# A one-layer decoder trunk: gates and branch projections with the tokens stationary, and squares and sums issued later

## The chip, the cores and the metric

One Trainium2 chip, one NeuronCore of it. The metric is the device time of one execution in microseconds, median of three runs. Inputs and outputs are float32.

## The reference, cut to what matters

One layer, 256 tokens, 2048 channels (`D_MODEL`), FFN width 5632. The mixer has two branches: A is gated linear attention over chunks, B a gated causal convolution with LayerNorm. Both are projected to 2048 channels, weighted by sigmoid gates computed from the input, added and projected once more.

```python
branch_a = (o * jax.nn.silu(r)) @ w_o_gla
...
u = jax.nn.silu(_layernorm(u, conv_norm_g, conv_norm_b))
branch_b = u @ w_pw2 + b_pw2
g_a, g_b = jnp.split(gates, 2, axis=-1)
merged = jax.nn.sigmoid(g_a) * branch_a + jax.nn.sigmoid(g_b) * branch_b
return merged @ w_out
...
h = h + _mixer(_rmsnorm(h, norm_mix[l]), ...)
h = h + (jax.nn.silu(y @ w_gate) * (y @ w_up)) @ w_down     # y = _rmsnorm(h, norm_ffn[l])
return _rmsnorm(h, norm_final)
```

## The kernel before, in words

**Split operands.** Every float32 operand of a large matmul is split into a high part (rounded to fp32r by ScalarE, line 194 or 815) and the rest (`lo`, a subtraction on VectorE, line 196 or 818); a product is hi·hi + lo·hi + hi·lo.

**Blocks of the mixer.** `run_blocks` (line 203) goes through the weight matrices in blocks of 512 output columns. A block has 16 row blocks of 128 input channels (K), loaded in 8 chunks of two. There are three forms of a product:

- Form "M" (lines 243 and 244): the weights are stationary, 128 columns at a time; the tokens stream. For each row block and each of four column groups there is one matmul of 512 columns (high and low part of the tokens, side by side) and one of 256 columns. The result has channels on partitions, and its two halves are added later (`merged_sum`, line 262: a ScalarE copy and a VectorE sum).
- Form "A" (lines 235 to 237): 128 tokens are stationary, 512 weight columns stream, three matmuls for each row block and each half of the tokens. The result has tokens on partitions. Before the change only the value projection uses it.
- Form "S" is for the narrow decay projection.

The order is: convolution values and gates (8 blocks), decay, keys, queries, values (4 blocks, form A), output gate `r` (4), gate A (4), gate B (4), branch A's projection (4, tokens `OG`, tile name `ogs`), branch B's projection (4, tokens `US`, tile `us`), output projection (4, tokens `MG`, tile `mgs`).

**What runs beside them.** Loading a chunk, and its cast and subtraction, are issued four chunks ahead (`LOOK`) by `load_next` (line 168); the weight loads go out on SP's queue. The element-wise work of attention and convolution waits in two lists, `gla_w_` and `conv_w_` (class `Work`, line 114). After each chunk `pump` (line 146) issues steps from them up to a budget. A step may have a delay in chunks, counted from the last step that its list issued (lines 126 and 127). Instructions here are not held in the written order: a scheduler places them by its own model of when their inputs are ready; `issue_after` only says behind which instruction a step may not come. Instructions wrapped in `kp` (`keep_in_program_order`) are held in order.

**The merge.** The gates' evacuation (`pair_evac`, line 485) applies the sigmoid; `o_evac` (line 688) multiplies branch A's projection by gate A; `pw_evac` (line 696) adds branch B's bias, multiplies by gate B, adds, and splits the merged channels (`MG`). The output projection reads row block k of `MG` in chunk k/2. `out_before` (line 708) closes the mixer's tile pools, opens the FFN's and loads the residual `XR` on SP's queue. `out_evac` (line 720) adds the residual, scales by the norm's gain, splits, and for every pair of 128-channel groups forms token sums (`token_sums`, line 769) and adds up squares (lines 738 to 743); at the end it folds them (line 747).

**The FFN.** It runs in steps of four row blocks of weights (`steps`, line 794): 88 for gate and up, 44 for down, most of them 24 matmuls of 512 columns with tokens stationary (lines 1228 to 1230); "S" steps use a seven-product scheme with more additions on VectorE. `run_ffn` (line 1185) writes the order out by hand: `vt["p"]` and `vt["d"]` model the time of TensorE and VectorE, `pump_d` (line 977) issues evacuations and preparations of later steps (a step has two halves, each with its cast and subtraction) when VectorE's modelled time is behind, and `turns` holds transposes with due times. `h2_norm` (line 1081) needs the folded squares; `h2_turn` (line 1090) transposes the residual, four 128x128 blocks at a time, through TensorE (line 1095). The down projection has two passes (`q` 0 and 1) over 1024 output columns each. At the end of a bank `dn_evac` (line 1102) adds the result to the residual (1105), squares it with a row sum on ScalarE (1108) and multiplies it by the final gain (1112).

Of the kernel before, what the change touches and what calls it, by code (L numbers as in the profile page):

```python
# [13 lines left out]
P = 128  # L14
T = 256
# [12 lines left out]
NPERS = 16  # L28
# [13 lines left out]
def trunk(ctx: ExitStack, tc, xT, par, convw, ws, wal2, nfin, out):  # L42
# [27 lines left out]
    def ptile(dt=F32, s="p"):  # L70
        return pers.tile([P, NB], dt, tag="p", name=nm(s))
# [87 lines left out]
    def add_block(width, nk, form, xs, evac, before=None, budget=BUD):  # L159
        blocks.append(dict(width=width, nk=nk, form=form, xs=xs, evac=evac,  # L160
                           before=before, budget=budget))
# [41 lines left out]
    def run_blocks():  # L203
# [11 lines left out]
        for b in blocks:  # L215
# [115 lines left out]
    def x_scaled(k):  # L331
        def f():
            s = ptile(F32R, "xs")
# [345 lines left out]
    MG = {}  # L679
# [7 lines left out]

    def o_evac(blk):
        def f(n, a):
            i = 4 * blk + n  # L690
            t = merged_sum(a)
            g = SGA[i // 2][:, i % 2, :]
            v.tensor_tensor(g, t, g, op=ALU.mult)
        return f

    def pw_evac(blk):
        def f(n, a):
            i = 4 * blk + n
            t = merged_sum(a, pcol(P_PB, i))
            u = ttile("mg")  # L700
            v.tensor_tensor(u, t, SGB[i // 2][:, i % 2, :], op=ALU.mult)
            w = ttile("mg2")
            v.tensor_tensor(w, u, SGA[i // 2][:, i % 2, :], op=ALU.add)
            MG[i] = ptile(F32R, "mgs")
            split(MG[i], w)
        return f

    def out_before(blk):
        def f():
            if blk == 0:  # L710
                mx.close()
                es = ctx.enter_context
                ffn["f"] = es(tc.tile_pool(name="fpool", bufs=NF, reuse_waits="tile"))
                ffn["x"] = es(tc.tile_pool(name="xpool", bufs=NX, reuse_waits="tile"))
            for i in range(2 * blk, 2 * blk + 2):
                XR[i] = atile([P, 2, T], s="xr")
                nc.sync.dma_start(XR[i], xT[:, 2 * i:2 * i + 2, :])
        return f

    def out_evac(blk):  # L720
        def f(n, a):
# [14 lines left out]
            if i % 2 == 1:  # L736
                token_sums(i // 2, YP.pop(i // 2))
                q = atile([P, 2, T], s="hq")
                sc.activation(q, H2[i // 2], AF.Square)
                if i > 1:  # L740
                    o = atile([P, 2, T], s="hss")
                    v.tensor_tensor(o, sums["h"], q, op=ALU.add)
                    q = o
                sums["h"] = q
# [24 lines left out]
    def token_sums(p, y):  # L769
        kinds = {k for w, _, q, k in gu if q == p}  # L770
        parts = []
        if "S" in kinds:
            f = atile([P, 4, P], s="sf")
            v.tensor_tensor(f[:, 0], y[:, 0, H1], y[:, 1, H1], op=ALU.subtract)
            v.tensor_tensor(f[:, 1], f[:, 0], y[:, 0, H0], op=ALU.subtract)
            v.tensor_tensor(f[:, 2], y[:, 0, H0], y[:, 0, H1], op=ALU.subtract)
            v.tensor_tensor(f[:, 3], y[:, 1, H0], f[:, 1], op=ALU.add)
            SY[p] = [atile([P, 4, P], F32R, "sy") for _ in range(2)]
            parts.append((f, *SY[p]))
        if "P" in kinds:  # L780
            f = atile([P, 2, P], s="df")
            v.tensor_tensor(f, y[:, :, H0], y[:, :, H1], op=ALU.subtract)
            DY[p] = atile([P, 2, 2, P], F32R, "dy")
            parts.append((f, DY[p][:, 0], DY[p][:, 1]))
        for f, hi, lo in parts:
            sc.copy(hi, f)
            v.tensor_tensor(lo, f, hi.bitcast(F32), op=ALU.subtract)
# [186 lines left out]
    evac = deque()  # L974
    turns = deque()
# [76 lines left out]
    def back(blk, n, x):  # L1052
# [9 lines left out]
        def cut(m):  # L1062
            hi, lo = HSV[blk, n] = ptile(F32R, "hsh"), ptile(F32R, "hsl")
# [26 lines left out]
    def h2_turn(th, nb):  # L1090
        def f():
# [4 lines left out]
            HTK[th, nb] = ptile(s="htk")  # L1096
# [5 lines left out]
    def dn_evac(q):  # L1102
        def add(t, nb, a, p0=0, p1=NB, c=None):
            h = HTK[t, nb]
            kp(v.tensor_tensor(h[:, p0:p1], a[:, p0:p1], h[:, p0:p1], op=ALU.add))
            sq = atile([P, NB], s="dq")
# [64 lines left out]
        def done_bank(b, a):  # L1171
# [8 lines left out]
            else:  # L1180
                later(0.7, lambda: add(t, nb, a))
                later(0.7, lambda: scaled(t, nb))
        return done_bank

    def run_ffn():
# [8 lines left out]
        while i < len(steps):  # L1194
# [89 lines left out]
    for blk in range(4):  # L1284
        add_block(NB, KT, "M", lambda: MG, out_evac(blk), before=out_before(blk))
# [62 lines left out]
```

## Time and profile before

| | |
|---|---|
| runs shown (3) | 1658.71, 1660.85, 1661.5 us; median 1660.85 |
| profiled execution | 1658.77 us, of it the span 1657.1 us |
| mean granted TensorE clock | 0.995 |
| TensorE / VectorE / ScalarE busy | 1640.4 / 1396.8 / 931.3 us |
| instructions | 22482 |
| DMA | 340.5 MB, mean 206 GB/s |

Times in the rows below are microseconds from the start of the span. A timeline row reads: start, duration, engine and line, operation, output<-inputs, size, count, and in brackets the engine's idle time before it with what ended it. Matmuls are pipelined, and their recorded durations overlap: the rate is read from starts. [...]

### The profile page before, as it was taken

How to read it: one execution, taken by the hardware profiler on the slowest of the kernel's cores; microseconds unless marked ns; L12 is line 12 of the kernel's file. 1: busy time of each engine (PE TensorE's matmuls, PEld its weight loads, DVE VectorE, ACT ScalarE, POOL GpSimd, SP SyncE). 2: the span in 40 equal slices, each digit the busy share in tenths (PEclk: the TensorE clock that was granted, in tenths of full speed). 3: DMA queues.
4: the chain of work that ended last, by engine and by line, in shares of the span. 5: the costliest groups of instructions: out<-in, count | busy, mean ns of one | idle time of the engine just before them, and what ended most of it. 6: DMA issues, size and time to landing. Idle time of an engine off the chain costs nothing.

```text
span 1657.1 us, 22482 instructions
## 1 busy us (share of the span) xinstructions
PE 1640.4 (99%) x8397; PEld 1394.6 (84%) x8397; DVE 1396.8 (84%) x2104; ACT 931.3 (56%) x1276; POOL 23.9 (1%) x46
## 2 busy tenths in 40 slices
PE   9999999999999999999999999999999999999997
PEld 8888888888888888888888888888888888887886
DVE  7998999888888889887668868888888888888776
ACT  6654444666666654475555555555555555544554
POOL 0000000000000000000000000000000000000000
PEclk9999999999999999999999999999999999999999
DMA  8555555554444545445556546666666767884963
GB/s 296 196 203 179 197 184 178 199 182 172 175 174 167 178 170 186 178 178 204 190 204 213 172 168 222 227 219 218 224 229 228 229 228 237 280 315 162 316 227 115
DMA packets 78365, 340.54 MB, mean 206 GB/s; under 512 B 8976, under 2 KB 10256, under 8 KB 58160
## 3 DMA queue, kind: packets, MB, share of 16 engines
q1 hardware_dynamic: 75232, 329.61, 57.1%
q0 software_dynamic: 2880, 9.44, 1.6%
q8 instruction: 65, 1.06, 0.3%
q14 instruction: 44, 0.36, 0.1%
q10 hardware_dynamic: 144, 0.07, 0.0%
HBM read 327.54 MB, written 11.53 MB: 205 GB/s over the span
## 4 chain that ended last, share of the span: by engine, by line
PE 94%; DVE 3%; DMA 1%; ACT 1%; issue 1%; ACTq 0%; SPq 0%; DVEq 0%
PE acc L243 32%; PE acc L244 16%; PE m L1229 13%; PE m L1230 13%; PE m L1228 13%; PE acc L235 2%; PE acc L236 2%; PE acc L237 2%; DVE lo L818 1%; DMA raw<-in_weights_dram 1%; PE m L1059 1%; PE m L596 0%; ACT hi L815 0%; PE m L511 0%; DMA pr<-in_par_dram 0%
## 5 line engine op out<-in xcount | busy, mean ns | idle before, releaser
L194 ACT CAST hi<-raw 128x1024 fp32r<-128x1024 f32 (+1 forms) x326 | 339.0, 1041 | 340.1 <-PE acc L243 280.1
L196 DVE TENSOR_TENSOR lo<-raw,hi 128x1024 fp32r<-128x1024 f32 (+1 forms) x326 | 393.4, 1208 | 110.2 <-ACT hi L194 107.9
L243 PE MATMUL acc<-xs,hi 128*128 128x512 f32 x1280 | 452.4, 398 | 0.0
L818 DVE TENSOR_TENSOR lo<-raw,hi 128x1024 fp32r<-128x1024 f32 x264 | 317.6, 1220 | 88.2 <-ACT hi L815 87.5
L244 PE MATMUL acc<-xs,lo 128*128 128x256 f32 x1280 | 359.0, 280 | 0.0
L815 ACT CAST hi<-raw 128x1024 fp32r<-128x1024 f32 x264 | 270.5, 1050 | 149.5 <-PE m L1230 72.4
L243 PEld LDWEIGHTS acc<-xs,hi 128*128 128x128 f32 x1280 | 240.3, 188 | 57.8 <-ACT hi L194 0.3
L244 PEld LDWEIGHTS acc<-xs,lo 128*128 128x128 f32 x1280 | 241.8, 189 | 0.1
L393 DVE SCALAR_TENSOR_TENSOR yc<-u,cw,yc 128x255 f32<-128x255 f32 (+14 forms) x480 | 199.5, 463 | 0.1
L1228 PE MATMUL m<-hi,y2s 128*128 128x512 f32 x404 | 159.4, 395 | 0.9 <-ACT hi L815 0.9
L1229 PE MATMUL m<-lo,y2s 128*128 128x512 f32 x404 | 157.8, 391 | 1.0 <-DVE lo L818 1.0
L1230 PE MATMUL m<-hi,y2s 128*128 128x512 f32 x404 | 157.9, 391 | 0.0
L243 PE MATMUL acc<-xu,hi 128*128 128x512 f32 x256 | 90.9, 398 | 1.1 <-DVE xu L107 1.1
L1229 PEld LDWEIGHTS m<-lo,y2s 128*128 128x128 f32 x404 | 76.2, 189 | 16.6 <-DVE lo L818 1.3
L1228 PEld LDWEIGHTS m<-hi,y2s 128*128 128x128 f32 x404 | 76.2, 188 | 16.5 <-ACT hi L815 1.3
L243 PE MATMUL acc<-ogs,hi 128*128 128x512 f32 x256 | 89.9, 395 | 0.0
L1230 PEld LDWEIGHTS m<-hi,y2s 128*128 128x128 f32 x404 | 76.1, 188 | 16.0
L243 PE MATMUL acc<-us,hi 128*128 128x512 f32 x256 | 88.8, 391 | 0.0
L243 PE MATMUL acc<-mgs,hi 128*128 128x512 f32 x256 | 88.8, 391 | 0.0
L1228 PE MATMUL m<-hi,hr 128*128 128x512 f32 x216 | 85.3, 395 | 2.6 <-ACT hi L815 2.6
L1229 PE MATMUL m<-lo,hr 128*128 128x512 f32 x216 | 85.5, 396 | 1.3 <-DVE lo L818 1.3
L1230 PE MATMUL m<-hi,hr 128*128 128x512 f32 x216 | 85.0, 394 | 0.0
(256 smaller groups left out, 2791.6 us busy)
## 6 DMA issues: line engine op xcount, KB each, us to landing
raw<-in_weights_dram SPq DMA_DIRECT2D x157, 1024.0 KB, 4.8
raw<-in_weights_dram SPq DMA_DIRECT2D x268, 512.0 KB, 4.9
hr<-hsd SPq DMA_DIRECT2D x56, 256.0 KB, 6.7
hsd<-hsh POOLq DMA_DIRECT2D x18, 256.0 KB, 2.7
hsd<-hsl POOLq DMA_DIRECT2D x18, 256.0 KB, 3.0
raw<-in_weights_dram SPq DMA_DIRECT2D x8, 256.0 KB, 4.7
xr<-in_xT_dram SPq DMA_DIRECT2D x8, 256.0 KB, 5.4
out_dram<-fin SPq DMA_DIRECT2D x8, 256.0 KB, 3.2
```

What stands on the lines that cost most here:

```text
L194: order["a"] = sc.copy(fl(hi), r).ins
L196: order["v"] = v.tensor_tensor(fl(lo), r, fl(hi).bitcast(F32), op=ALU.subtract).ins
L235: pe.matmul(a, lhsT=xh, rhs=hi[:, kk, :], start=st, stop=False)
L236: pe.matmul(a, lhsT=xh, rhs=lo[:, kk, :], start=False, stop=False)
L243: pe.matmul(a, lhsT=wh, rhs=x, start=st, stop=False)
L244: last = pe.matmul(a[:, T:2 * T], lhsT=wl, rhs=xh, start=False, stop=en)
L393: v.scalar_tensor_tensor(y[:, d:T], in0=u_tile(i)[:, 0:T - d], scalar=cw[:, i, CW - 1 - d:CW - d], in1=y[:, d:T], op0=ALU.mult, op1=ALU.add)
L815: kp(sc.copy(dst, src))
L818: kp(v.tensor_tensor(dst, src, hi.bitcast(F32), op=ALU.subtract))
L1228: kp(pe.matmul(a, lhsT=xh, rhs=wh, start=st, stop=False))
L1229: kp(pe.matmul(a, lhsT=xh, rhs=wl, start=False, stop=False))
L1230: kp(pe.matmul(a, lhsT=xl, rhs=wh, start=False, stop=en))
```

## The change

The eight gate blocks and the eight blocks of the two branch projections go from form M to form A. The gates' sigmoid reads the accumulator directly, 512 wide; the two branches are merged with tokens on partitions. Branch B's bias, now needed along the free axis, is rearranged once by a GpSimd transfer into a DRAM row (`brow`) and broadcast to all partitions, 512 values per block. The merged result is transposed back by TensorE, four 128x128 blocks into one PSUM bank, copied by ScalarE and split by VectorE (`turn_merged`). `out_before` of the first output block is called ahead of the last two chunks instead of at the block's start. In the FFN's start the last pair's squares, the fold and the last two pairs' token sums go into a list `slow` with due times on TensorE's modelled time; in the first pass of the down projection the square and the final scaling go there too. Tiles of the long-lived pool are made twice as large and half as many.

```diff
-NPERS = 16
+NPERS = 8
...
     def ptile(dt=F32, s="p"):
-        return pers.tile([P, NB], dt, tag="p", name=nm(s))
+        return pers.tile([P, 2, NB], dt, tag="p", name=nm(s))
...
             for c in range(nch):
+                if c == nch - 2 and b["late"]:
+                    b["late"]()
...
-    MG = {}
+    class Merged(dict):
+        def __missing__(self, k):
+            gla_w_.drain(("mg", k // 4))
+            return self[k]
+    MG = Merged()
+    BP = {}
+    brow = dpool.tile([16, P], F32, tag="brow", name="brow")
+    with nc.allow_non_contiguous_dma(reason="2048 values once"):
+        nc.gpsimd.dma_start(brow, par[:, P_PB:P_PB + 16].rearrange("p i -> i p"))
+
+    def sg_evac(store):
+        def mk(blk):
+            def f(n, a):
+                store[n, blk] = atile([P, NB], s="sg")
+                sc.activation(store[n, blk], a, AF.Sigmoid)
+            return f
+        return mk
+
     def o_evac(blk):
         def f(n, a):
-            i = 4 * blk + n
-            t = merged_sum(a)
-            g = SGA[i // 2][:, i % 2, :]
-            v.tensor_tensor(g, t, g, op=ALU.mult)
+            g = SGA[n, blk]
+            v.tensor_tensor(g, a, g, op=ALU.mult)
+        return f
+
+    def pw_before(blk):
+        def f():
+            if blk == 0:
+                conv_w_.drain("conv")
+            BP[blk] = atile([P, NB], s="bp")
+            nc.sync.dma_start(BP[blk], brow[4 * blk:4 * blk + 4, :].rearrange("a b -> (a b)").partition_broadcast(P))
         return f
 
     def pw_evac(blk):
         def f(n, a):
-            i = 4 * blk + n
-            t = merged_sum(a, pcol(P_PB, i))
-            u = ttile("mg")
-            v.tensor_tensor(u, t, SGB[i // 2][:, i % 2, :], op=ALU.mult)
-            w = ttile("mg2")
-            v.tensor_tensor(w, u, SGA[i // 2][:, i % 2, :], op=ALU.add)
-            MG[i] = ptile(F32R, "mgs")
-            split(MG[i], w)
+            u = SGB[n, blk]
+            t = atile([P, NB], s="mg")
+            v.tensor_tensor(t, a, BP[blk], op=ALU.add)
+            v.tensor_tensor(u, t, u, op=ALU.mult)
+            v.tensor_tensor(u, u, SGA[n, blk], op=ALU.add)
+            if n == 1:
+                for z in range(2):
+                    turn_merged(blk, z)
+                gla_w_.mark(("mg", blk))
         return f
 
+    def turn_merged(blk, z):
+        st = {}
+
+        def t():
+            m = st["m"] = misc()
+            for j in range(2):
+                for n in range(2):
+                    pe.transpose(m[:, (2 * j + n) * P:(2 * j + n + 1) * P],
+                                 SGB[n, blk][:, (2 * z + j) * P:(2 * z + j + 1) * P], ident)
+
+        def cut():
+            mg = ptile(F32R, "mgs")
+            m = st["m"].rearrange("p (k t) -> p k t", k=2)
+            sc.copy(mg[:, :, 0:T], m)
+            v.tensor_tensor(mg[:, :, T:2 * T], m, mg[:, :, 0:T].bitcast(F32), op=ALU.subtract)
+            for j in range(2):
+                MG[4 * blk + 2 * z + j] = mg[:, j]
+        gla_w_.add(0.0, t, 1 if z else 3)
+        gla_w_.add(0.7, cut, 1)
+
     def out_before(blk):
         def f():
             if blk == 0:
+                gla_w_.drain(("mg", 3))
                 mx.close()
...
             if i % 2 == 1:
-                token_sums(i // 2, YP.pop(i // 2))
-                q = atile([P, 2, T], s="hq")
-                sc.activation(q, H2[i // 2], AF.Square)
...
-            if i == 15:
-                fo = ttile("hf")
-                v.tensor_tensor(fo, sums["h"][:, 0, :], sums["h"][:, 1, :], op=ALU.add)
-                sums["f"] = fo
+                def square():
+                    q = atile([P, 2, T], s="hq")
+                    kp(sc.activation(q, H2[i // 2], AF.Square))
...
+                def fold():
+                    sums["f"] = ttile("hf")
+                    kp(v.tensor_tensor(sums["f"], sums["h"][:, 0, :], sums["h"][:, 1, :], op=ALU.add))
+                if i < 13:
+                    token_sums(i // 2, YP.pop(i // 2))
+                if i < 15:
+                    square()
+                else:
+                    slow.extend([(1.0, square), (1.5, fold)] + [
+                        (5.0 + 3.0 * z, lambda p=p: token_sums(p, YP.pop(p))) for z, p in enumerate((6, 7))])
...
         def add(t, nb, a, p0=0, p1=NB, c=None):
             h = HTK[t, nb]
             kp(v.tensor_tensor(h[:, p0:p1], a[:, p0:p1], h[:, p0:p1], op=ALU.add))
+            if q:
+                square(t, nb, p0, p1, c)
+            else:
+                slow.append((vt["p"] + 12.0 + 6.0 * len(slow), lambda: (square(t, nb), scaled(t, nb))))
...
                 later(0.7, lambda: add(t, nb, a))
-                later(0.7, lambda: scaled(t, nb))
+                if q:
+                    later(0.7, lambda: scaled(t, nb))
...
             for z in range(len(groups[0])):
...
+                if slow and slow[0][0] <= vt["p"]:
+                    slow.popleft()[1]()
+                    vt["d"] += 0.7
...
-    ga = pair_evac(SGA, AF.Sigmoid, "sga")
+    ga, gb = sg_evac(SGA), sg_evac(SGB)
     for blk in range(4):
-        add_block(NB, KT, "M", xx, ga(blk), before=layernorm if blk == 0 else None)
-    gb = pair_evac(SGB, AF.Sigmoid, "sgb")
+        add_block(NB, KT, "A", xx, ga(blk), before=layernorm if blk == 0 else None)
     for blk in range(4):
-        add_block(NB, KT, "M", xx, gb(blk))
+        add_block(NB, KT, "A", xx, gb(blk))
     for blk in range(4):
-        add_block(NB, KT, "M", lambda: OG, o_evac(blk),
+        add_block(NB, KT, "A", lambda: OG, o_evac(blk),
...
     for blk in range(4):
-        add_block(NB, KT, "M", lambda: US, pw_evac(blk),
-                  before=(lambda: conv_w_.drain("conv")) if blk == 0 else None)
+        add_block(NB, KT, "A", lambda: US, pw_evac(blk), before=pw_before(blk))
     for blk in range(4):
-        add_block(NB, KT, "M", lambda: MG, out_evac(blk), before=out_before(blk))
+        add_block(NB, KT, "M", lambda: MG, out_evac(blk), **{"before" if blk else "late": out_before(blk)})
```

In the token sums (`token_sums`) the instructions are now wrapped in `kp`.

## Rows read from the trace of the kernel before

**Rows 1.** The page: busy time, share and instructions by engine; the chain by engine.

```profile
PE 1640.4 (99%) x8397; PEld 1394.6 (84%) x8397; DVE 1396.8 (84%) x2104; ACT 931.3 (56%) x1276; POOL 23.9 (1%) x46
...
PE 94%; DVE 3%; DMA 1%; ACT 1%; issue 1%; ACTq 0%; SPq 0%; DVEq 0%
```

**Rows 2.** Timeline of TensorE in a gate stage, form M, three pairs apart.

```profile
599.63 0.40 PE L243 MATMUL acc<-xs,hi 128*128 128x512 f32 x1
...
600.69 0.40 PE L243 MATMUL acc<-xs,hi 128*128 128x512 f32 x1
```

**Rows 3.** Timeline of TensorE: first matmul of branch A's, branch B's and the output projection.

```profile
663.59 0.40 PE L243 MATMUL acc<-ogs,hi 128*128 128x512 f32 x1
...
753.85 0.39 PE L243 MATMUL acc<-us,hi 128*128 128x512 f32 x1
...
842.60 0.39 PE L243 MATMUL acc<-mgs,hi 128*128 128x512 f32 x1
```

**Rows 4.** Timeline of TensorE in the value projection, form A, six matmuls apart.

```profile
299.68 0.39 PE L236 MATMUL acc<-lo,xs 128*128 128x512 f32 x1
...
301.04 0.39 PE L236 MATMUL acc<-lo,xs 128*128 128x512 f32 x1
```

**Rows 5.** Timeline of VectorE and TensorE where the mixer hands over to the FFN.

```profile
940.04 0.28 DVE L776 TENSOR_TENSOR sf<-yp 128x128 f32<-128x128 f32 x1
940.25 0.28 DVE L775 TENSOR_TENSOR sf<-sf,yp 128x128 f32<-128x128 f32 x1
...
941.81 0.69 DVE L787 TENSOR_TENSOR sy<-sf,sy 128x512 fp32r<-128x512 f32 x1 [0.74 <-ACT sy L786]
...
942.04 0.39 PE L1230 MATMUL m<-hi,dy 128*128 128x512 f32 x1
...
943.29 0.49 PE L1228 MATMUL m<-hi,y2s 128*128 128x512 f32 x1 [0.87 <-ACT hi L815]
...
943.48 1.22 DVE L818 TENSOR_TENSOR lo<-raw,hi 128x1024 fp32r<-128x1024 f32 x1
...
944.75 0.50 PE L1229 MATMUL m<-lo,y2s 128*128 128x512 f32 x1 [0.96 <-DVE lo L818]
```

**Rows 6.** Timeline of TensorE around four transposes; their group by line (busy, mean ns).

```profile
949.20 0.39 PE L1230 MATMUL m<-hi,y2s 128*128 128x512 f32 x1
949.43 0.60 PE L1095 MATMUL m<-ident,h 128*128 128x128 f32 x4
...
950.10 0.40 PE L1229 MATMUL m<-lo,y2s 128*128 128x512 f32 x1
...
L1095 PE MATMUL m<-ident,h 128*128 128x128 f32 x32 | 4.8, 272 | 0.0
```

**Rows 7.** Windows: length, busy PE, PEld, DVE, ACT, POOL; granted clock, DMA share, GB/s.

```profile
945.00:949.00 4.00, 4.00 (x14) 3.29 (x14) 4.00 (x4) 3.58 (x5) 0.00 (x0) 0.57 0.47 163
```

**Rows 8.** Timeline of TensorE and ScalarE between the down projection's two passes.

```profile
1525.97 0.39 PE L1230 MATMUL m<-hi,hr 128*128 128x512 f32 x1
...
1527.20 0.63 ACT L1108 ACTIVATE dq<-htk 128x512 f32<-128x512 f32 x1 [1.36 <-DVE htk L1105]
...
1527.83 1.98 ACT L815 CAST hi<-raw 128x1024 fp32r<-128x1024 f32 x2
...
1528.91 0.64 PE L1228 MATMUL m<-hi,hr 128*128 128x512 f32 x1 [2.56 <-ACT hi L815]
...
1530.17 0.80 PE L1229 MATMUL m<-lo,hr 128*128 128x512 f32 x1 [0.62 <-DVE lo L818]
```

**Rows 9.** Windows at the same place, columns as in rows 7.

```profile
1526.00:1530.00 4.00, 1.00 (x3) 0.19 (x1) 2.97 (x4) 2.60 (x4) 0.00 (x0) 0.89 0.02 7
1530.00:1536.00 6.00, 5.83 (x14) 4.57 (x15) 4.97 (x7) 3.55 (x5) 0.00 (x0) 0.51 0.58 186
```

**Rows 10.** First 25 us: the chain (start, duration); a DMA queue's packets, MB, share.

```profile
10.74 6.29 DMA raw<-in_weights_dram
...
q10 hardware_dynamic: 144, 0.07, 0.9%
```

More of the change, by code (lines that the diff above doesn't have):

```diff
@@ L70, in ptile, with phalf @@
     def ptile(dt=F32, s="p"):
-        return pers.tile([P, NB], dt, tag="p", name=nm(s))
+        return pers.tile([P, 2, NB], dt, tag="p", name=nm(s))
+    pair_of = {}
+    def phalf(i, dt=F32, s="p"):
+        if i % 2 == 0:
+            pair_of[s] = ptile(dt, s)
+        return pair_of[s][:, i % 2]
     def misc(shape=(P, 512)):
@@ L157, in trunk, with add_block @@
     blocks = []
-    def add_block(width, nk, form, xs, evac, before=None, budget=BUD):
+    def add_block(width, nk, form, xs, evac, before=None, budget=BUD, late=None):
         blocks.append(dict(width=width, nk=nk, form=form, xs=xs, evac=evac,
-                           before=before, budget=budget))
+                           before=before, budget=budget, late=late))
     loads = []
@@ L332, in f @@
         def f():
-            s = ptile(F32R, "xs")
+            s = phalf(k, F32R, "xs")
             t = ttile("xn")
@@ L736, in f @@
             if i % 2 == 1:
-                token_sums(i // 2, YP.pop(i // 2))
-                q = atile([P, 2, T], s="hq")
-                sc.activation(q, H2[i // 2], AF.Square)
[L740 to L744, printed above, removed]
-            if i == 15:
-                fo = ttile("hf")
-                v.tensor_tensor(fo, sums["h"][:, 0, :], sums["h"][:, 1, :], op=ALU.add)
-                sums["f"] = fo
+                def square():
+                    q = atile([P, 2, T], s="hq")
+                    kp(sc.activation(q, H2[i // 2], AF.Square))
+                    if i > 1:
+                        o = atile([P, 2, T], s="hss")
+                        kp(v.tensor_tensor(o, sums["h"], q, op=ALU.add))
+                        q = o
+                    sums["h"] = q
+                def fold():
[8 more added lines that the diff above has]
+                        (5.0 + 3.0 * z, lambda p=p: token_sums(p, YP.pop(p))) for z, p in enumerate((6, 7))])
         return f
@@ L773, in token_sums @@
             f = atile([P, 4, P], s="sf")
[L774 to L777, printed above, removed]
+            kp(v.tensor_tensor(f[:, 0], y[:, 0, H1], y[:, 1, H1], op=ALU.subtract))
+            kp(v.tensor_tensor(f[:, 1], f[:, 0], y[:, 0, H0], op=ALU.subtract))
+            kp(v.tensor_tensor(f[:, 2], y[:, 0, H0], y[:, 0, H1], op=ALU.subtract))
+            kp(v.tensor_tensor(f[:, 3], y[:, 1, H0], f[:, 1], op=ALU.add))
             SY[p] = [atile([P, 4, P], F32R, "sy") for _ in range(2)]
@@ L781, in token_sums @@
             f = atile([P, 2, P], s="df")
-            v.tensor_tensor(f, y[:, :, H0], y[:, :, H1], op=ALU.subtract)
+            kp(v.tensor_tensor(f, y[:, :, H0], y[:, :, H1], op=ALU.subtract))
             DY[p] = atile([P, 2, 2, P], F32R, "dy")
@@ L785, in token_sums @@
         for f, hi, lo in parts:
-            sc.copy(hi, f)
-            v.tensor_tensor(lo, f, hi.bitcast(F32), op=ALU.subtract)
+            kp(sc.copy(hi, f))
+            kp(v.tensor_tensor(lo, f, hi.bitcast(F32), op=ALU.subtract))
     gu = [("gu", b, p, "S" if p in SEVEN[b] else "P") for b in range(11) for p in range(8)]
@@ L974, in trunk @@
     evac = deque()
+    slow = deque()
     turns = deque()
@@ L1062, in cut @@
         def cut(m):
-            hi, lo = HSV[blk, n] = ptile(F32R, "hsh"), ptile(F32R, "hsl")
+            hs = ptile(F32R, "hs")
+            hi, lo = HSV[blk, n] = hs[:, 0], hs[:, 1]
             cast(hi, m)
@@ L1095, in f @@
                 kp(pe.transpose(m[:, q * P:(q + 1) * P], H2[i // 2][:, i % 2, th * P:(th + 1) * P], ident))
-            HTK[th, nb] = ptile(s="htk")
+            HTK[th, nb] = phalf(nb, s="htk")
             kp(sc.copy(HTK[th, nb], m))
@@ L1105, in add, with square @@
             kp(v.tensor_tensor(h[:, p0:p1], a[:, p0:p1], h[:, p0:p1], op=ALU.add))
+            if q:
+                square(t, nb, p0, p1, c)
+            else:
+                slow.append((vt["p"] + 12.0 + 6.0 * len(slow), lambda: (square(t, nb), scaled(t, nb))))
+        def square(t, nb, p0=0, p1=NB, c=None):
+            h = HTK[t, nb]
             sq = atile([P, NB], s="dq")
```

## The prediction

> **What bounds the kernel now.** I read the page's busy shares and its chain of waits first. TensorE is busy nearly all the span and carries 94% of the chain [rows 1]: the time is TensorE's issue time plus the few places where TensorE stands still. So I priced issue rates from the timeline of TensorE (starts of successive matmuls, since the recorded durations overlap), and then looked for its idle entries.
>
> Issue rates. In the M form a pair is one 512-column and one 256-column matmul. In the two gate stages three pairs take 1.06 us, 0.353 us a pair [rows 2]. In the branch B projection 256 pairs run from 753.85 to 842.60, 0.347 a pair [rows 3]. The kernel thus issues the same pair at two speeds; the trace does not say why. The A form already exists here, in the value projection, inside the slower of those stretches: six matmuls of 512 columns from 299.68 to 301.04, 0.2267 us each [rows 4]. Per row block of weights the two forms stream the same columns (4 x 768 = 6 x 512), but M issues 8 instructions and A 6.
>
> Standstills. There are two of any size. [...] Where the first half of the down projection ends, it waits again, at 1528.91 and 1530.17 [rows 8], and from 1530 to 1536 the granted clock is 0.51, the lower level almost throughout [rows 9].
>
> **The change part by part.** The profiled execution took 1658.77 us (span 1657.1); the median of the three runs is 1660.85, 2.1 above it. I sum against the former and add 2.1.
>
> *Sixteen blocks from M to A* (two gates, two branch projections; four blocks of sixteen row blocks each). An A block is 96 x 0.2267 = 21.76 us. The eight gate blocks: 8 x 64 x 0.353 = 180.9 becomes 174.1, a gain of 6.8. Branch B: 88.75 becomes 87.05, 1.7. Branch A: 90.26 from 663.59 to 753.85 [rows 3] becomes 87.05 plus the two small LayerNorm reductions that stand in it in both kernels; I leave 1.0 for them (bounds 0 and 1.5) and take 2.2. **Sum -10.7.**
>
> *Thirty-two transposes* of 128x128 are new, eight groups of four. The FFN already has such groups: from 949.20 to 950.10, one group between two matmuls took 0.90 us where two matmul steps alone take 0.45, so 0.45 a group [rows 6]. **+3.6.** Each group brings a ScalarE copy and a VectorE subtraction 512 wide (0.69 us, as the operation at 941.81 [rows 5]), and what they replace is more: per block the M form spent four copies, four sums and, in the last projection, four 256-wide splits. They lie under TensorE: the last projection block's channels are first read in the seventh chunk of the output projection, 6 x 2.77 = 16.6 us after the block ends (88.75 us are 32 chunks). Without that cover TensorE would wait for two groups' work, some 5 us, once.
>
> By the rows a group in the stream costs 0.45 us, though each transpose's recorded duration is 272 ns [rows 6]. [...] I follow the spacing.
>
> *Where the transposes stand on TensorE.* They read what VectorE finishes only after the block's last matmul (three 512-wide operations of 0.69 us for each token half), and the code can add them right behind that matmul: the written delay of three chunks counts from the queue's last step, which is long past. I price this at 0.5 us in all, since the program's scheduler does not keep written order: VectorE ran line 776 before line 775 [rows 5]. From below it is 0; from above see the first rival.
>
> *First standstill.* TensorE lost 1.25 + 1.45 - 0.45 = 2.25 us [rows 5], and (1 - 0.57) x 4 = 1.7 at the lower clock [rows 7]. What was late was the cast at the head of the third FFN step, which stands on ScalarE behind the squares; the subtraction stands on VectorE behind the token sums, the sum of squares and its fold (941.81 to 943.48 [rows 5]). The change puts the squares, fold and both last token sums behind that step's first half. About 3 us of VectorE work leaves the chain, so the subtraction should end near 942 where it now starts at 943.48, and TensorE needs it two matmul steps after 942.04, at 942.5. Next late would be the tiny norm matmuls, which need the fold some 1.4 us after that; VectorE has it by about 943.2. **-3.9.**
>
> *Second standstill.* The cast at 1527.83 starts as the third square with its accumulator read ends (1527.20) [rows 8]: ScalarE takes them in order, and each scaling on VectorE waits for its square too. The change leaves only the four additions there; squares and scalings come one by one 12 to 30 us later. The cast then runs as soon as it has data and a buffer. No transfer is late next: DMA was idle in that gap (share 0.02 [rows 9]). Gain: from 1525.97 to 1530.17 there are 4.2 us for two steps of 0.227, so 3.75 lost, and (1 - 0.51) x 6 = 2.9 at the lower clock. **-6.6.** The moved work, four squares of 0.63 us and four scalings of 0.69, goes under later steps of 5 us each; its cover is TensorE's stream there, without it VectorE's 2.8 us would be on the path. I count it within the 0.5 above.
>
> *The bias row.* A GpSimd transfer turns 2048 values one by one at the start, where TensorE's chain hangs on weight loads (one took 6.29 us [rows 10]). The nearest row is the parameter load: 144 packets held 0.9% of sixteen engines over 25 us, 25 ns each [rows 10]. At that price 2048 pieces take 3.2 us of every engine. From below 0 (the engines have pauses), from above 3.2 if all of it delays the loads, more if a piece costs more than a row of 512 B. I take the middle, **+1.5**. The four broadcast loads and the later x loads on SP's queue have most of a block in hand: 0.
>
> *The output projection* keeps the M form, and may run at 0.347 as now or at 0.353: 0 to 1.7 us, taken as **+0.8**.
>
> Sum: -10.7 + 3.6 + 0.5 - 3.9 - 6.6 + 1.5 + 0.8 = -14.8; 1658.8 - 14.8 = 1644.0, as a median 1646.
>
> **The rivals.**
> 1. *The transposes wait at the head of TensorE's queue* (slower). If the written order holds, each branch B block ends with TensorE waiting for the second half's three operations (2.1), what is left of the first half's (0.7, since that half ends six steps of 0.227 earlier) and perhaps a weight subtraction (1.22 [rows 5]): 4.0 us, four times. The first standstill, of 2.25 us, was followed by 1.7 us lost to the clock. 4 x 5.7 = 22.8 gives 1668. It turns the sign once the wait with its clock loss exceeds 14.8 / 4 = 3.7 us a block. For: the delay that does not bind. Against: the reordering in [rows 5].
> 2. *The second standstill stays*, because VectorE is late itself: 1646 + 6.6 = 1652.6. For: it was busy 2.97 of the 4 us around it [rows 9]. Against: the first idle entry names the cast, not VectorE [rows 8], and part of that busy time is the scalings that go.
> 3. *The start is delayed* by 2048 pieces at several times 25 ns: three times that price is 9.6 us, 8 more than counted, 1654. For: the chain there is DMA [rows 10]. Against: no row shows a dear small piece.
> 4. *Transposes at their full duration*: 1646 + 5.2 = 1651. For: the 272 ns. Against: the 0.90 us in the stream. [...]
>
> **How the numbers follow.** Forecast 0.63, rival 1 0.10, rival 2 0.14, rival 3 0.08, rival 4 0.05. A measurement of this kernel can tell about 0.2%, 3.3 us. Faster by more than that is below 1657.5: the forecast, rivals 2 and 4 and nearly all of 3, 0.88. Of rival 1, where the wait may be shorter, 0.08 is slower; what is left, 0.04, is the same. Low end: bias row, projection speed and small waits at nothing, -2.8, and 1 us for the bounds in branch A, 1642. High end 1655 takes in rivals 2 to 4 and leaves out rival 1.
>
> **What would show it.** Right: starts 0.227 apart in gates and projections; four-transpose groups at 0.45 without idle before them; no idle entry above 0.5 us where the FFN begins, nor where the second half of the down projection begins; no granted clock under 0.95 at either place. Wrong: idle entries that name VectorE before transposes; the weight load at the start that lands at 17.03 [rows 10] landing later; a wait for a cast near 1515 to 1525 in place of that at 1528.

## The result, and the profile after

The changed kernel takes **1680.74 us** (median of 4 runs, 1677.8 to 1683.3) against 1660.8 us for the kernel before: a ratio of 1.0126 with the 95% interval [1.011, 1.0142]. It is 20 us slower, where 1646 us and a range up to 1655 us were forecast. Its profiled execution took 1679.42 us (span 1677.7). All differences below are against the profiled execution of before.

The page of the changed kernel, the lines that answer to [rows 1]: busy time, share and instructions by engine, then the chain by engine.

```profile
PE 1641.9 (98%) x7917; PEld 1376.0 (82%) x7917; DVE 1377.6 (82%) x2016; ACT 908.4 (54%) x1188; POOL 25.3 (2%) x47
...
PE 91%; DVE 4%; DMA 2%; issue 1%; ACT 1%; SPq 0%; ACTq 0%; DVEq 0%
```

TensorE issues 480 instructions fewer and VectorE has less to do, as the diff says, and still the span is 20.65 us longer. TensorE's share of the chain fell from 94 to 91%, so the time went into standing still. Where it did is read from the first matmul of each stage; after − before gives what a stage gained or lost. The timeline of TensorE, changed kernel (start, duration, engine and line, operation):

```profile
10.52 0.79 PE L251 MATMUL acc<-xu,hi 128*128 128x512 f32 x1 [4.77 <-DVE xu L115]
...
111.06 0.40 PE L251 MATMUL acc<-xs,hi 128*128 128x512 f32 x1
...
670.69 0.39 PE L243 MATMUL acc<-hi,ogs 128*128 128x512 f32 x1
...
758.64 0.39 PE L243 MATMUL acc<-hi,us 128*128 128x512 f32 x1
...
865.16 0.48 PE L251 MATMUL acc<-mgs,hi 128*128 128x512 f32 x1
...
957.93 0.40 PE L1307 MATMUL m<-hi,y2s 128*128 128x512 f32 x1
...
1435.03 0.39 PE L1307 MATMUL m<-hi,hs 128*128 128x512 f32 x1
```

The third block of the first stage, which begins here at 111.06 us, began in the kernel before at:

```profile
98.20 0.39 PE L243 MATMUL acc<-xs,hi 128*128 128x512 f32 x1
```

The same rows for all kernels of this study, as the length of each stage in us (differences of first matmuls in each one's profiled execution; e1 to e8 are the experiments below):

| stage | before | after | e1 | e2 | e3 | e4 | e5 | e6 |
|---|---|---|---|---|---|---|---|---|
| start to the third block of the first stage | 98.20 | 111.06 | 98.51 | 118.24 | 115.19 | 99.03 | 98.94 | 100.41 |
| from there to branch A (gates in it) | 565.39 | 559.63 | 559.63 | 559.63 | 559.63 | 559.63 | 565.40 | 559.63 |
| branch A's projection | 90.26 | 87.95 | 87.95 | 87.95 | 87.94 | 87.95 | 90.26 | 87.95 |
| branch B's projection | 88.75 | 106.52 | 104.83 | 89.89 | 104.98 | 89.89 | 88.74 | 87.04 |
| output projection | 88.75 | 92.77 | 92.79 | 91.32 | 92.85 | 91.32 | 88.75 | 90.44 |
| FFN up to the down projection | 476.80 | 477.10 | 475.26 | 476.94 | 472.88 | 472.91 | 478.53 | 472.99 |
| down projection to the last matmul | 239.98 | 233.50 | 233.42 | 233.41 | 233.43 | 233.41 | 233.44 | 233.52 |

In the column of after, three stages did about what was forecast: the gates gain 5.8 us, branch A's projection 2.3, the down projection 6.5. Three did not, and the trace names a place for each.

**The start**, 12.9 us later. The first 25 us of the changed kernel as DMA issues (output<-input, queue, count, KB of one, median us from issue to landing), and a queue's packets, MB and share of the engines:

```profile
q1 hardware_dynamic: 2444, 3.48, 88.5%
q0 software_dynamic: 48, 0.01, 3.8%
...
raw<-in_weights_dram SPq DMA_DIRECT2D x8, 256.0 KB, 8.5
...
brow<-in_par_dram POOLq DMA_DIRECT2D x1, 8.0 KB, 17.0
```

The same first 25 us of the kernel before:

```profile
q1 hardware_dynamic: 3531, 6.91, 84.3%
...
raw<-in_weights_dram SPq DMA_DIRECT2D x8, 256.0 KB, 4.7
```

The queue of the weight and x loads holds the engines as long as before and moves half as much: a 256 KB load lands after 8.5 us instead of 4.7, and the bias row's 8 KB take 17.0 us, although its own packets (queue q0) hold the engines for 3.8% of the time only. The chain of these 25 us has one weight load of 16.43 us in it, and the windows show how little the compute engines do meanwhile (length, busy PE, PEld, DVE, ACT, POOL, granted clock as a share of full speed, DMA share, GB/s):

```profile
5.00:10.00 5.00, 0.75 (x4) 0.46 (x3) 1.17 (x3) 0.62 (x2) 0.00 (x0) 0.95 1.26 29
10.00:15.00 5.00, 2.93 (x8) 2.13 (x8) 0.47 (x2) 0.00 (x0) 0.00 (x0) 0.50 1.03 62
15.00:20.00 5.00, 0.00 (x0) 0.00 (x0) 0.72 (x2) 1.37 (x3) 0.00 (x0) 0.50 0.80 181
```

In the first two windows the DMA share is 1.26 and 1.03 at only 29 and 62 GB/s. TensorE is busy for 0.75, 2.93 and 0.00 of each 5 us up to 20 us, and behind its first idle stretch (4.77 us, up to 10.52) its granted clock is 0.50.

**Branch B's projection**, 17.8 us longer, and the output projection, 4.0. The timeline of TensorE at the end of the first branch B block:

```profile
780.17 0.39 PE L245 MATMUL acc<-hi,us 128*128 128x512 f32 x1
783.25 0.33 PE L752 MATMUL m<-ident,sg 128*128 128x128 f32 x1 [2.69 <-DVE sg L737]
783.33 0.48 PE L243 MATMUL acc<-hi,us 128*128 128x512 f32 x1
...
784.11 0.59 PE L752 MATMUL m<-ident,sg 128*128 128x128 f32 x3
```

VectorE in the same stretch, and a window behind it:

```profile
778.96 1.23 DVE L204 TENSOR_TENSOR lo<-raw,hi 128x1024 fp32r<-128x1024 f32 x1 [1.50 <-ACT hi L202]
780.11 1.28 DVE L735 TENSOR_TENSOR mg<-acc,bp 128x512 f32<-128x512 f32 x2
781.30 1.28 DVE L736 TENSOR_TENSOR sg<-mg,sg 128x512 f32<-128x512 f32 x2
782.51 1.29 DVE L737 TENSOR_TENSOR sg<-sg,sg 128x512 f32<-128x512 f32 x2
```
```profile
784.00:788.00 4.00, 4.00 (x14) 3.21 (x13) 1.62 (x2) 0.59 (x1) 0.00 (x0) 0.57 0.26 83
```

The first transpose stands ahead of the next block's matmuls on TensorE and waits for the merged tile. VectorE takes both token halves' additions, then both multiplications, then both last additions, so even the first half is ready only after five of the six. 780.17 to 783.25 are 3.08 us for one step of 0.23, so 2.85 us lost, and then the granted clock is 0.57 over 4 us: (1 - 0.57) x 4 = 1.7 us more. Three of the group's four transposes were moved behind three matmuls by the program's scheduler; one in front is enough. The four blocks together, from the changed kernel's view of the tile (time until, number of waits):

```profile
DVE sg L737: 10.9, 4
```

**The hand-over to the FFN**, no gain. TensorE, VectorE and a window of the changed kernel, against [rows 5] and [rows 7]:

```profile
968.60 0.39 PE L1309 MATMUL m<-hi,dy 128*128 128x512 f32 x1
970.46 0.50 PE L1307 MATMUL m<-hi,y2s 128*128 128x512 f32 x1 [1.47 <-ACT hi L881]
971.72 0.50 PE L1308 MATMUL m<-lo,y2s 128*128 128x512 f32 x1 [0.76 <-DVE lo L884]
```
```profile
967.48 0.69 DVE L800 TENSOR_TENSOR hss<-hss,hq 128x512 f32<-128x512 f32 x1
968.20 0.42 DVE L806 TENSOR_TENSOR hf<-hss 128x256 f32<-128x256 f32 x1
968.55 0.42 DVE L848 TENSOR_TENSOR df<-yp 128x256 f32<-128x256 f32 x1
969.49 0.43 DVE L853 TENSOR_TENSOR dy<-df,dy 128x256 fp32r<-128x256 f32 x1 [0.53 <-ACT dy L852]
970.43 1.23 DVE L884 TENSOR_TENSOR lo<-raw,hi 128x1024 fp32r<-128x1024 f32 x1 [0.52 <-ACT hi L881]
```
```profile
972.00:976.00 4.00, 4.00 (x14) 3.30 (x14) 3.31 (x6) 3.37 (x4) 0.00 (x0) 0.57 0.02 4
```

The moved operations, the sum of squares, its fold and a token sum, still stand ahead of the weight subtraction that TensorE needs (970.43): the entries of the slow list came due too early.

### The profile page after: what moved, and what is told of

Same layout as the page of the kernel before. It is cut to its first block, busy times and chain, and to the rows that moved or that the text cites. A ratio compares the mean times of both kernels' runs of the same rounds, so it can differ in the third digit from the quotient of the medians.

```text
span 1677.7 us, 21315 instructions
## 1 busy us (share of the span) xinstructions
PE 1641.9 (98%) x7917; PEld 1376.0 (82%) x7917; DVE 1377.6 (82%) x2016; ACT 908.4 (54%) x1188; POOL 25.3 (2%) x47
## 4 chain that ended last, share of the span: by engine, by line
PE 91%; DVE 4%; DMA 2%; issue 1%; ACT 1%; SPq 0%; ACTq 0%; DVEq 0%
PE acc L251 17%; PE m L1308 12%; PE m L1309 12%; PE m L1307 12%; PE acc L252 9%; PE acc L243 9%; PE acc L244 9%; PE acc L245 9%; DMA raw<-in_weights_dram 2%; DVE lo L884 1%; PE m L1126 1%; DMA xr<-in_xT_dram 0%; PE m L606 0%; ACT hi L202 0%; DVE mg L735 0%
## 5 line engine op out<-in xcount | busy, mean ns | idle before, releaser
L251 PE MATMUL acc<-xs,hi 128*128 128x512 f32 x768 | 270.3, 397 | 0.0
L252 PE MATMUL acc<-xs,lo 128*128 128x256 f32 x768 | 215.4, 281 | 0.0
L251 PEld LDWEIGHTS acc<-xs,hi 128*128 128x128 f32 x768 | 144.1, 188 | 34.9 <-ACT hi L202 0.3
L243 PE MATMUL acc<-hi,xs 128*128 128x512 f32 x384 | 151.3, 394 | 0.0
L245 PE MATMUL acc<-hi,xs 128*128 128x512 f32 x384 | 149.5, 389 | 0.0
L244 PE MATMUL acc<-lo,xs 128*128 128x512 f32 x384 | 149.5, 389 | 0.0
L252 PEld LDWEIGHTS acc<-xs,lo 128*128 128x128 f32 x768 | 145.1, 189 | 0.0
L251 PE MATMUL acc<-mgs,hi 128*128 128x512 f32 x256 | 92.2, 404 | 0.0
L243 PEld LDWEIGHTS acc<-hi,xs 128*128 128x128 f32 x384 | 72.1, 188 | 15.3 <-issue 0.7
```

The source lines that it names most:

```text
L243: pe.matmul(a, lhsT=xh, rhs=hi[:, kk, :], start=st, stop=False)
L244: pe.matmul(a, lhsT=xh, rhs=lo[:, kk, :], start=False, stop=False)
L245: last = pe.matmul(a, lhsT=xl, rhs=hi[:, kk, :], start=False, stop=en)
L251: pe.matmul(a, lhsT=wh, rhs=x, start=st, stop=False)
L252: last = pe.matmul(a[:, T:2 * T], lhsT=wl, rhs=xh, start=False, stop=en)
```

## The experiments

The theory had three parts: the element-wise bias transfer holds up the start, the transposes wait at the head of TensorE's queue, and the slow list's due times are too small. The rivals are in each expectation. The first four ran together, beside the kernel before at 1658.63 us.

**e1: the bias row later.** The same transfer, after the last work of GpSimd that the mixer needs.

```diff
     def layernorm():
         tmp = {}
+        with tc.issue_after(order["g"]), nc.allow_non_contiguous_dma(reason="2048 values once"):
+            nc.gpsimd.dma_start(brow, par[:, P_PB:P_PB + 16].rearrange("p i -> i p"))
...
-        nc.gpsimd.dma_start(brow, par[:, P_PB:P_PB + 16].rearrange("p i -> i p"))
...
```

> The changed kernel with the GpSimd transfer of the 2048 bias values issued at the start of the gate stages instead of at the start of the kernel; nothing else moves. Theory A (the 2048 four-byte pieces hold the DMA engines while the first weight and x loads are on the chain): the first matmul is back near 6.7 us, the third convolution block begins near 98 us instead of 111, total 12.9 us less than the changed kernel, about 1668; the transfer takes about as long where it now stands, and there it costs nothing or little, since loads run several chunks ahead. Rival (the transfer costs its 12 to 13 us wherever it stands): total stays near 1681, with idle TensorE in the gate stages. Rival (the start is late for another reason, such as the doubled long-lived tiles): first matmul still after 10 us.

Measured: 1666.12 us (1663.28 to 1666.95), ratio 1.0043 [1.0028, 1.0058], 14.6 us less than the changed kernel. The start is back (98.51); the waits at the transposes and at the hand-over are still there. No stage behind the start is more than 1.9 us from after's. The two that differ, branch B's projection by 1.69 us and the FFN's first stage by 1.84, are shorter by about the 1.7 us that the clock cost after each wait in after: behind the first of the four transposes' waits the granted clock is 1.00, as this window shows, and behind the hand-over it is the stage's length that says so.

```profile
770.90:775.00 4.10, 4.10 (x21) 3.36 (x21) 2.17 (x3) 1.41 (x2) 0.00 (x0) 1.00 0.37 148
```

GpSimd issues the transfer at 434.39 us. The window from 440 to 450 us, and the loads' queue and issues from 430 to 450 us:

```profile
434.39 1.17 POOL L416 DMA_DIRECT2D brow<-in_par_dram  x1
...
440.00:450.00 10.00, 10.00 (x59) 8.69 (x58) 8.15 (x13) 7.83 (x11) 0.00 (x0) 1.00 0.16 13
...
q1 hardware_dynamic: 304, 2.23, 37.7%
...
raw<-in_weights_dram SPq DMA_DIRECT2D x3, 1024.0 KB, 9.0
```

The kernel before, 430 to 450 us:

```profile
q1 hardware_dynamic: 474, 3.49, 47.2%
...
raw<-in_weights_dram SPq DMA_DIRECT2D x3, 1024.0 KB, 4.7
```

The pieces hold up the loads here too. The load issued just before them, at 434.20 us, lands after 4.9 us, but the next, at 442.38, lands after 12.0, where the kernel before has 4.7 at that place; from 440 to 450 us the queue moves 13 GB/s, before 144. It costs nothing here: loads are issued four chunks ahead, and TensorE is busy all of those 10 us at full clock. So the pieces hold up the other queue here as at the start; what differs is whether TensorE waits for the very next load.

**e2: the transposes' delay made to bind.** The queue's last step is set to now, so that the written three chunks count from the block's end.

```diff
             if n == 1:
+                gla_w_.last = tick[0]
                 for z in range(2):
                     turn_merged(blk, z)
```

> The changed kernel with the delay of three chunks counted from the moment at which the transposes are put into the list, so that they stand on TensorE two chunks behind the block whose result they read. Theory B (TensorE stood 3 us before the first transpose of each of four blocks, waiting for VectorE's three operations, and ran 3.4 us at half clock after each): no idle entry before the transposes, granted clock 1.00 in branch B's projection and at the start of the output projection, branch B's projection about 90 us instead of 106.5, the output projection shorter by some 1 to 2, total about 18 us less, 1663. Rival (the transposes are dear in themselves, or they break the clock): the four half-clock stretches stay and the gain is at most the 4 x 2.8 us of waiting, 1670. Rival (the wait only moves to the output projection, whose first chunks need the merged channels): a new idle entry there, gain under 10 us.

Measured: 1665.32 us (1664.28 to 1668.29), ratio 1.0044 [1.0029, 1.0059], 15.4 us less. In its profile the two projections are 18.1 us shorter than after (16.6 and 1.5); the start happened to be 7.2 us later in that execution. TensorE's timeline at the first group:

```profile
792.79 0.39 PE L245 MATMUL acc<-hi,us 128*128 128x512 f32 x1
793.02 0.60 PE L753 MATMUL m<-ident,sg 128*128 128x128 f32 x4
793.38 0.48 PE L243 MATMUL acc<-hi,us 128*128 128x512 f32 x1
793.69 0.40 PE L244 MATMUL acc<-lo,us 128*128 128x512 f32 x1
```

Four transposes without idle time before them. The granted clock is 1.00 from 765.80 to 855.70, the whole of branch B's projection, and the output projection takes the 91.32 us that it takes in e4, at 1.00 too. The whole loss there was the wait and what it did to the clock: 2.85 and 1.7 us, four times, are 18.2.

**e3: the slow list later.**

```diff
-                    slow.extend([(1.0, square), (1.5, fold)] + [
-                        (5.0 + 3.0 * z, lambda p=p: token_sums(p, YP.pop(p))) for z, p in enumerate((6, 7))])
+                    slow.extend([(5.0, lambda: (square(), fold()))] + [
+                        (10.0 + 3.0 * z, lambda p=p: token_sums(p, YP.pop(p))) for z, p in enumerate((6, 7))])
```

> The changed kernel with later due times in the list of slow steps: the last square and its fold together at 5.0, the token sums at 10 and 13, so that the first half of the third FFN step is cast and split ahead of all of them. Theory C (the first standstill stayed because VectorE's modelled time already holds the four halves prepared ahead, 4.9 us, so that entries due at 1.0, 1.5 and 5.0 are issued ahead of that half): the waits for cast and split at 970.5 and 971.7 (2.7 us) and the 3.4 us at half clock go, a wait of up to 0.5 us for the fold may come, total about 4 us less, 1677. Rival (the half is late because of the residual evacuation alone): the wait stays above 1.5 us, total same as the changed kernel.

Measured: 1677.89 us (1677.82 to 1678.09), ratio 1.0117 [1.01, 1.0134]: 2.9 us less than the changed kernel, and 4.2 us in the stage (477.10 to 472.88). Again the start was later in that execution (115.19 against 111.06). TensorE where the norm's small matmuls come, and a window over the whole hand-over:

```profile
972.62 0.39 PE L1309 MATMUL m<-hi,y2s 128*128 128x512 f32 x1
973.04 0.58 PE L1152 MATMUL m<-ones,hf 128*128 128x1 f32 x4
973.48 0.47 PE L1307 MATMUL m<-hi,y2s 128*128 128x512 f32 x1
```
```profile
960.00:985.00 25.00, 24.96 (x126) 20.49 (x125) 17.94 (x35) 14.37 (x24) 0.00 (x0) 1.00 0.42 140
```

No idle entry is left, and the norm still finds its fold in time. The first standstill goes as soon as the moved work really stands behind the weight pieces.

**e4: all three.** The edits of e2 and e3, and the bias row read from its own input, which is contiguous, so that the GpSimd transfer falls away:

```diff
...
-            nc.sync.dma_start(BP[blk], brow[4 * blk:4 * blk + 4, :].rearrange("a b -> (a b)").partition_broadcast(P))
+            nc.sync.dma_start(BP[blk], bpw[blk * NB:(blk + 1) * NB].partition_broadcast(P))
...
```

> The changed kernel with the bias given as a contiguous row of 2048 values that is broadcast directly (no element-wise transfer at all), the transposes' delay as in e2 and the due times as in e3. If the three causes are separate, the gains add: 12.9 + 18 + 4 = 35 us less than the changed kernel, about 1645.5, which is also the time that the sum of the prediction gives without the three faults. If they overlap (a start or a wait that another wait hides), 1648 to 1655.

Measured: **1645.14 us** (1644.08 to 1645.93), ratio 0.9919 [0.9904, 0.9934]. It is faster than both kernels. A window over nearly the whole of it:

```profile
5.00:1635.00 1630.00, 1626.26 (x7899) 1364.75 (x7897) 1375.13 (x2008) 903.63 (x1180) 23.59 (x40) 1.00 0.61 208
```

TensorE is busy 1626.26 of 1630 us, at full clock.

The next four ran together, beside the kernel before at 1659.5 us (17 runs, 1657.34 to 1662.3).

**e5: the down projection's deferral alone, in the kernel before.**

```diff
+            if q:
+                square(t, nb, p0, p1, c)
+            else:
+                slow.append((vt["p"] + 12.0 + 6.0 * len(slow), lambda: (square(t, nb), scaled(t, nb))))
...
+                if slow and slow[0][0] <= vt["p"]:
+                    slow.popleft()[1]()
+                    vt["d"] += 0.7
```

> The kernel before with the down projection's deferral alone: sums of squares and scalings of its first six blocks come from the slow list, while the last two token sums and the hidden squares stay in their old place. Theory (the second standstill was VectorE and ScalarE work behind which the lookahead's pieces stood, and it needs nothing of the merge): the stage from the down projection to the last matmul falls from 239.98 us to 233.5 us, nothing else moves, the first standstill stays, and the kernel takes 1652.2 us. Rival (the standstill goes only together with the other parts): the stage stays at 240 us and the kernel at 1658.6 us.

Measured: 1654.21 us (1651.39 to 1657.66), ratio 0.9967 [0.9956, 0.9978]. The stage is 233.44 us, to 0.1 us what the theory said; the deferral needs nothing of the merge. The kernel gained 5.3 us and not 6.5: in the profiled execution the FFN's first stage is 1.7 us longer, though nothing in it was edited. It is the first standstill, which is still there; this window follows it.

```profile
945.50:952.30 6.80, 6.79 (x20) 5.63 (x21) 4.57 (x5) 3.83 (x5) 0.00 (x0) 0.50 0.66 203
```

The granted clock is 0.50 over these 6.8 us, 3.4 lost, where over the 4 us of [rows 7] it was 0.57, 1.7 lost. The same wait, 0.88 and 0.95 us of idle time here and 0.87 and 0.96 in [rows 5], cost more of the clock this time.

**e6: no transposes.** In e4, ScalarE and VectorE read the merged tile instead of the transposed bank; the transposing is left out.

```diff
-            m = st["m"] = misc()
-            for j in range(2):
-                for n in range(2):
-                    pe.transpose(m[:, (2 * j + n) * P:(2 * j + n + 1) * P],
-                                 SGB[n, blk][:, (2 * z + j) * P:(2 * z + j + 1) * P], ident)
+            st["m"] = SGB[z, blk]
```

> The kernel with all three faults taken out, without the 32 transposes: ScalarE and VectorE read the merged tile itself instead of the transposed bank, so the merged channels stay untransposed and what follows is computed on the wrong order of elements. Theory (a transpose costs the step from one to the next, about 0.11 us, as the groups of the trace show): 8 groups at 0.45 us, 1645.1 - 3.6 = 1641.5 us. Rival (each costs its whole recorded duration, 0.272 to 0.275 us, and takes from the clock behind it): 32 x 0.275 = 8.8 us, 1636.3 us or less.

Measured: 1642.03 us (1639.73 to 1642.89), ratio 0.9893 [0.9878, 0.9908], 3.1 us below e4 by the medians. The stages say it more closely: branch B's projection 89.89 to 87.04, the output projection 91.32 to 90.44, together 3.73 us for eight groups, 0.47 a group. That is 0.12 us for a transpose; its recorded 272 ns are not its price.

**e7 and e8: what of the transfer holds up the start.** To e4, which needs no such transfer, one is added that nobody reads, at the place of the change's own: in e7 the same 8 KB as 16 rows of 512 B, in e8 half the pieces.

```diff
...
+        nc.gpsimd.dma_start(brow, bpw.rearrange("(a b) -> a b", a=16))
```
```diff
...
+        nc.gpsimd.dma_start(brow[0:8, :], par[:, P_PB:P_PB + 8].rearrange("p i -> i p"))
```

> The kernel with all three faults taken out, which reads the bias row from the input directly, with one more transfer that nobody reads: at the place where the change has its own, on the same GpSimd queue, the same 8192 B into the same tile, but in 16 whole rows of 512 B instead of 2048 pieces of 4 B. Theory (the pieces hold up the start): the start stays, first large matmul at 6.6 us, third convolution block at 98.5 to 99.0 us, kernel 1645.1 us. Rival (any transfer on the GpSimd queue beside the first loads does it): third convolution block at 111 us or later, kernel 1658 us.

> The same kernel, with a transfer of half the pieces that nobody reads: 1024 pieces of 4 B into 8 partitions of the tile, at the place where the change has its own, on the same queue. Theory (the cost goes with the number of pieces): about half of 12.9 us, third convolution block near 105 us, kernel 1651.5 us. Rival A (a fixed cost as soon as the loads stand beside such pieces): third convolution block at 111 us or later, kernel 1658 us. Rival B (half of it fits beside the loads): the start as without, kernel 1645.1 us.

Measured: e7 1646.07 us (1645.06 to 1646.79), ratio 0.9919 [0.9902, 0.9935]; e8 1654.99 us (1653.46 to 1656.67), ratio 0.9973 [0.9964, 0.9982]. The third block of the first stage begins at 99.84 and 108.61 us (e4: 99.03). The issues of e7 in the first 25 us:

```profile
raw<-in_weights_dram SPq DMA_DIRECT2D x8, 256.0 KB, 4.9
...
brow<-in_b_pw_dram POOLq DMA_DIRECT2D x1, 8.0 KB, 3.7
```

And of e8, with a window:

```profile
raw<-in_weights_dram SPq DMA_DIRECT2D x8, 256.0 KB, 9.6
...
brow<-in_par_dram POOLq DMA_DIRECT2D x1, 4.0 KB, 16.1
```
```profile
10.00:15.00 5.00, 1.88 (x8) 1.23 (x8) 0.22 (x1) 0.00 (x0) 0.00 (x0) 0.66 0.63 34
```

Same queue, same place, same bytes: as rows the transfer costs under 1 us, as pieces it holds up the start. Half the pieces land after 16.1 us and cost 9.6 us of start against e4. All of them land after 17.0, 24.2 and 21.8 us in the profiled executions of after, e2 and e3, and cost 12.0, 19.2 and 16.2 us of start against e4. So the price varies from one execution to the next, and half the pieces cost less than all of them in any of the three. A fixed price is out: e8's ten runs all lie below the 1658 us that it would give. Half for half would be 6.0 to 9.6 us by these three; e8 lies at the upper end of that, so the rule stays open.

## Why the prediction was wrong, and where it was right

The sum was 1644.0 us for the profiled execution; it took 1679.42, 35.4 more. Three steps make 33 of them:

1. **The bias row** was put at 1.5 us and cost 12.9: 11.4 us. The price of a piece came from packets that carry a row each, 25 ns; the step said the cost would be more "if a piece costs more than a row of 512 B", and then took the middle of bounds that left that out. Rival 3 named it and gave it three times the price and a chance of 0.08; even that was short. What failed is deeper than the price: the step counted the engines' time on the row's own packets, 3.2 us of every engine; the trace records 3.8% of 25 us, 0.95, and the loss is in the loads, of which one of 256 KB lands after 8.5 us instead of 4.7. By e1 the same pieces hold up the loads at 434 us too, where those are not needed at once and no time is lost; by e7 the same bytes in rows cost under 1 us at the start.
2. **Where the transposes stand on TensorE** was put at 0.5 us and cost 18.1 (e2): 17.6 us. Rival 1 happened, in its place and by its mechanism, with 2.85 us of waiting and 1.7 of clock a block where it had 4.0 and 1.7. That is above the 3.7 us a block at which it was to turn the sign, and e1, which has only this fault and the next, is indeed slower than before. The step had seen that the written delay does not bind, and set it aside because the scheduler had once swapped two VectorE operations of 0.28 us. That row shows that it reorders, not that it moves a waiting instruction behind a block. It did move three of four transposes, by three matmuls.
3. **The first standstill** was to give back 3.9 us and gave none: with the 0.3 by which the stage grew, 4.2 us. The price was right, since e4's stage is 3.9 us shorter than before. The premise was not: "the change puts the squares, fold and both last token sums behind that step's first half". It puts them behind due times of 1.0 to 8.0 us in the planner's modelled time; by its code, four weight halves of 1.22 us are already planned on VectorE when the FFN starts, so that most of the list comes due ahead of the third step's pieces. That count is read from the code; the trace shows three of the four entries (sum of squares, fold, one token sum) ahead of the subtraction at 970.43. e3, which changes only the due times and makes square and fold one entry, brings the step back.

Of the other terms, the eight gate blocks gave 5.8 us for 6.8 and the output projection cost 1.7 for 0.8, together 1.9 more. The rest were right:

- *Branch A and B*: 2.3 us for 2.2; branch B without its transposes (e6) 1.71 for 1.7.
- *Transposes*: 0.47 us a group for 0.45. Rival 4 is out: in e2 too the recorded duration of one is 272 ns (median of 32), but as a price in a stream the spacing in e2 and the difference of e4 and e6 decide, 0.11 to 0.12 us each. No run shows rival 4's 5.2 us: 32 times 272 ns are 8.7 us, 5.1 more than the 3.6 counted, and the 32 cost 3.73 us in all. Four at a time among matmuls left the granted clock at 1.00 in branch B's projection of e2.
- *Second standstill*: 6.5 us for 6.6, in every kernel that has the deferral and, by e5, without the rest. Rival 2 is out. A smaller wait of 0.71 us for a weight subtraction, earlier in the first pass, stays as it was in the kernel before.

That e4 comes out at 1645.1 us, within 1 us of the 1646 forecast, is a sum of terms that hold with two that cancel (gates and output projection up 1.9, the 0.5 for waits and 1.5 for the row not needed); it shows that the prediction was of the kernel that the change was meant to be, and not of the one that its order and due times make.

## What to carry to other kernels

Where an instruction of a new kind goes on the engine that sets the time, work out from the code what stands in front of it and behind it, and price the wait as if written order held, clock included; a scheduler's reordering counts only as far as a row shows it for that queue. Due times in a planner's model are worth nothing until one has computed what the model's clocks hold when the list is filled. And a transfer of many tiny pieces, here 2048 of 4 B, is judged by the loads that come behind it: the same one held them up at 434 us (12.0 us to landing instead of 4.7) as it did at the start (8.5 instead of 4.7), but cost nothing where they run chunks ahead, and 12.0 to 19.2 us where TensorE waits for the next one.

## What the runs showed of the hardware

- **The pieces held up the loads' queue.** In the first 25 us the loads' own packets took as much of the engines for 3.48 MB as for 6.91 MB without the pieces (88.5% and 84.3%). In e7, where the same 8 KB go as 16 rows, they took 82.4% for 6.83 MB, and the start is 0.81 us later than in e4. What in the engines holds the loads is not shown: the trace records the pieces' own packets at 3.8% of the engines. At 434 us (e1) the loads were held too, at 13 GB/s from 440 to 450 us where before has 144. How the price goes with the number of pieces stays open.
- **The wait's price in clock varied.** At the FFN, behind a wait of 2.25 us in before, the granted clock was 0.57 over 4 us, 1.7 us lost; behind one of 2.28 in e5 it was 0.50 over 6.8 us, 3.4 lost; in e1 the stage is 2.35 us longer than in e4, which leaves next to nothing for the clock beside the wait. Behind the four waits at the transposes, 2.85 to 2.93 us each, it fell four times in after, with 1.7 us lost each time (0.57 from 784 to 788 us, 0.66 from 811 to 816, 0.72 from 838 to 844, 0.57 from 866 to 870); in e1 and e3 branch B's projection is 1.69 and 1.54 us shorter, about one such loss. So in these runs a standstill of two to three us cost between 1.0 and 2.5 times its length.
- **One pair, two speeds.** The M form's pair of matmuls took 0.347 or 0.353 us for whole stages on end, and which stage has which changed with the edits: the output projection went from 88.75 us (0.347 a pair) to 90.44 (0.353) in e6, where TensorE has no new instruction in it. No run shows the cause; it moves such a forecast by 1.7 us a stage.
